# Small products of two heads, issued in turn on the two halves of the TensorE array

## The chip, the cores and the metric

The kernel runs on one core of a Trainium2 chip. The metric is device time in microseconds (us) of one execution; lower is better. Times of before are the median of three executions, and the profile is of one more execution of the same program.

## The reference

A decoder trunk of two layers on 256 tokens of 1024 features, in float32. Layer 0 mixes tokens with four heads of gated linear attention (GLA, chunked, keys of 64, values of 128) and eight heads of sparse attention (DSA: an indexer scores the keys, the best 64 of each token are kept, then softmax attention with a relative bias), and is followed by a dense SwiGLU. Layer 1 mixes with eight FoX heads (softmax attention with a forget bias) and eight dilated heads, and is followed by a SwiGLU of eight experts of which each token takes two. Every sub-layer ends in a norm.

```python
y = x @ w_in                                  # one projection for all heads of a layer
s = einsum('bqhd,bkd->bhqk', q_idx, k_idx)    # DSA indexer, 8 heads of 64
logits = einsum('bqhd,bkhd->bhqk', q, k) * dh ** -0.5 + bias     # 3 x 8 heads of 64
o = einsum('bhqk,bkhd->bqhd', softmax(logits), v)
A = einsum('bhtk,bhsk,bhtsk->bhts', qi, ki, decay)               # GLA within a chunk
x = LN(ALPHA * x + concat(heads) @ w_out)
```

## The kernel before

Every weight matrix is streamed in pieces of up to 1 MB on SP's queue, and ScalarE and VectorE split each piece into two float32r parts (`piece`, L165 and L167). Each large product is then three matmuls, L193 to L195 (`mm3`). The small products of the token mixers work on float32 directly, and every such matmul shows in the trace as two TensorE instructions.

A head has 64 features. Two heads, an even and an odd one, lie above each other in the 128 partitions: the even one in rows 0 to 63, the odd one in rows 64 to 127. So a product over 64 features uses one half of the rows of the array (the trace writes its shape 64\*128), and the two heads of a pair use different halves. The product of the weights with the values contracts over 128 keys and has 64 results, so it uses half of the columns (128\*64).

- `scores` (L538) forms the scores of one head: token tile 0 against 128 keys, token tile 1 against 256 keys, both into one PSUM bank. It is called for each of the 8 heads of the indexer in `dsa_select` (L551) and for each of the 8 heads of the three attentions (L374).
- `attention` (L365) is a generator of eleven steps. Step i forms the scores and the softmax of head i (`weights`: VectorE adds the bias, L666, L749 or L753; maximum L379; exponential L380 and scaling L384 on ScalarE), transposes the weights of head i - 2 (L389, and a ScalarE copy, L391, into one of two buffers `PT`), and multiplies head i - 3 with its values (`values`, L398 and L400). The two heads of a pair share one bank `pos`, which is copied out by `split` (L187, L188) after the odd one. The weights `L` have four buffers.
- `gla_scores` (L427) forms nine sets of products, each for two head pairs d and the two heads a of each: one of q and k themselves, one for b = 128 (L489) and seven levels (L460). `level` does all products of head a = 0 into one bank and copies them out under a mask (L466), then does the same for head a = 1 with another bank.

PSUM has two pools of four banks: `bank` for the large products and `abank` for everything else, so scores, transposes, values and GLA levels share four.

The order on each engine is fixed when the program is built: a planner goes through the instructions with the order of the source as their priority and a timeline of estimated costs, and takes what it holds to be ready, so the small products are put between pieces of large ones. Where a buffer is not yet free, an instruction is put later. The stages of a mixer are woven by hand: `interleave` of the projections with `gla_scores` and `dsa_select` (L650), `weave` of the last projections with GLA's output and the DSA attention (L671, L673), `interleave` of two projections with the FoX attention (L760), and the dilated attention with nothing beside it but the output projection (L766). In `out_proj` the last blocks of token tile 1 are held behind those of tile 0, so that they cover its norm.

Of the kernel before, what the change touches and what calls it, by code (L numbers as in the profile page):

```python
# [18 lines left out]
PSUM = bass.MemoryType.PSUM  # L19
# [3 lines left out]
S = 256  # L23
NT = 2
# [11 lines left out]
# ---------------------------------------------------------------- constants of the shapes  # L36
# [8 lines left out]
def shape_constants():  # L45
    """Masks, permutations and bucket one-hots; none of them depends on the data."""
# [24 lines left out]
def layouts(inputs):  # L71
    """gain and bias of the norm before the router, a feature per partition"""
    cols = np.stack([inputs["ln_g"][1, 0], inputs["ln_b"][1, 0]]).reshape(2, KT, 128).transpose(2, 0, 1)
    return {"ln_cols": np.ascontiguousarray(cols)}
# [13 lines left out]
def interleave(main, side, n=1, m=1):  # L88
    """emit n steps of main, m steps of side, and so on"""
    alive = [True, True]  # L90
    while any(alive):
        for i, g, k in ((0, main, n), (1, side, m)):
            for _ in range(k):
                if alive[i] and next(g, g) is g:
                    alive[i] = False


def weave(pattern, **gens):
    """emit one step of the generator that each letter of the pattern names"""
    for c in pattern:  # L100
        next(gens[c], None)


def lead(n, k):
    """order of the products of n blocks with two token tiles: the first tile ends k blocks before the second"""
# [3 lines left out]
class Trunk:  # L109
# [14 lines left out]
    # ---------------------------------------------------------------- helpers  # L124
    def widen_ring(self, ctx, name, n, later=False):
        """n more buffers for the weights; if later, only once the function that is returned has been called"""
# [15 lines left out]
    def piece(self, src, later=False, cuts=2, raw=None):  # L142
        """Stream one piece of a weight matrix ([128, n, w], or several such side by side) and split it exactly into two float32r parts.
        Returns part(j, columns) -> pair of [128, columns] for the j-th of the n blocks; if later, also a function
        that makes the first part of the i-th of the cuts, which share the blocks evenly, and returns one for the second."""
# [30 lines left out]
    def ring(self, w, dtype=F32):  # L176
        """next buffer of the ring that the weights arrive in"""
# [4 lines left out]
    def rows(self, w, k0, n, c0, c1):  # L182
        """rows k0*128.. of a matrix as [128, n, c1-c0]"""
# [6 lines left out]
    def mm3(self, out, a, b, start, stop):  # L190
        """out += a^T b with a, b pairs of float32r parts"""
# [5 lines left out]
    def proj_t(self, src, evacs, xT):  # L197
        """transposed projection of a piece of columns, up to 128 columns for each of evacs:
        evac(psum [columns, 256 tokens])"""
# [10 lines left out]
    def heads_t(self, w, c0, dst, xT, scale=None, step=2):  # L210
        """transposed projection of all groups of dst ([128, groups, 256]), `step` of them per piece"""
# [4 lines left out]
    def proj_n(self, w, c0, wd, xT, evac):  # L216
        """natural projection of wd (<=512) columns: evac(token tile, psum [128, wd])"""
# [15 lines left out]
    def transposed(self, dst, x, t):  # L233
        """x[:, t] ([128, 1024]) -> dst[:, :, 128 tokens of tile t] (pair of float32r parts)"""
# [8 lines left out]
    def ln_params(self, layer, sub, gb=None):  # L243
        """gain and bias of a norm on all partitions"""
# [7 lines left out]
    def residual_norm(self, x, t, ys, gb, tap=None):  # L252
        """x[:, t] = LN(ALPHA * x[:, t] + y), y given as two halves in PSUM, which are overwritten;
        tap(t, statistics) sees the input of the norm in x[:, t]"""
# [14 lines left out]
    def normalise(self, x, t, st, gb, us, out=None):  # L269
        """x[:, t] = (x - mu) / sqrt(var + eps) * g + b, with the sums of the two halves in st[:, 0:2];  # L270
        us: room for two halves; out: where the result goes to in DRAM"""
# [17 lines left out]
    # ---------------------------------------------------------------- set-up  # L289
# [29 lines left out]
    def router_weights(self):  # L319
        """The router works on z, the input of its norm LN(z) = (z - mu) * rstd * g + b:  # L320
        LN(z) wr = (z (g wr) - mu sum(g wr)) * rstd + b wr, with sums over the features"""
# [16 lines left out]
    def bias_tables(self, m):  # L338
        """Toeplitz bias [128, 8, 256] for the DSA heads and for the dilated heads, t - s = 128 + p - n"""
# [15 lines left out]
    def bias_expand(self, pool, scr, w, name):  # L355
        """T[p, h, n] = row[h, 127 - p + n]"""
# [7 lines left out]
    # ---------------------------------------------------------------- attention  # L364
    def attention(self, qT, kT, v, logits, oT, kt0):  # L365
        """softmax attention of 8 heads of 64; logits(h, S, L) forms the biased and masked logits L from S,
        both [128, 384] = token tile 0 (128 keys) | token tile 1 (256 keys). qT already holds 1/sqrt(d).
        Writes oT[:, kt0:kt0+4] (pair of float32r parts)."""
        nc = self.nc
        blk = (slice(0, 128), slice(128, 384))  # L370
        Ls, PTs, pos = {}, {}, {}

        def weights(h):
            p = self.scores(qT, kT, slice((h % 2) * 64, (h % 2) * 64 + 64), h // 2, h // 2)  # L374
# [18 lines left out]
        def values(h):  # L393
            hp, a = divmod(h, 2)
            if a == 0:
                pos[hp] = self.abank()
            o, PT = pos[hp][a * 64:(a + 1) * 64, :], PTs[h]
            nc.tensor.matmul(o[:, 0:256], v[:, 0, h * 64:(h + 1) * 64], PT[:, 0:256],  # L398
                             start=True, stop=False, skip_group_check=True)
            nc.tensor.matmul(o[:, 128:256], v[:, 1, h * 64:(h + 1) * 64], PT[:, 256:384],  # L400
                             start=False, stop=True, skip_group_check=True)
            if a == 1:
                self.split(oT[0][:, kt0 + hp], oT[1][:, kt0 + hp], pos[hp][:, :S])

        for i in range(8 + 3):
# [4 lines left out]
            if 0 <= i - 3 < 8:  # L410
                values(i - 3)
            yield

    # ---------------------------------------------------------------- GLA
    def logsig(self, z, w, scale=None):
        """log(sigmoid(z)) of a PSUM/SBUF block [128, w] into a new tile"""
# [10 lines left out]
    def gla_scores(self, gaT, q, k, AT, AO):  # L427
        """q, k: [128 (2 heads), 2, 256] transposed; forms A^T (two token tiles) and the off-diagonal block"""
# [22 lines left out]
        def level(X, Y, mask, b):  # L451
            """products of all rows of X with the later halves of the blocks of Y, kept where the mask is set"""
            later = lambda v: v.rearrange("p (m c) -> p m c", c=2 * b)[:, :, b:] if b else v
            n = 64 if b else 128
            for a in range(2):
                r = slice(a * 64, a * 64 + 64)
                p = self.abank()
                for t in range(NT):
                    for d in range(2):
                        nc.tensor.matmul(p[:, (2 * t + d) * n:(2 * t + d + 1) * n],  # L460
                                         X[r, d, t * 128:(t + 1) * 128], later(Y[r, d, t * 128:(t + 1) * 128]),
                                         start=True, stop=True)
# [11 lines left out]
        for i, b in enumerate((128,) + GLA_LEVELS):  # L474
# [9 lines left out]
            if b == 128:  # L484
                for a in range(2):
                    r = slice(a * 64, a * 64 + 64)
                    p = self.abank()
                    for d in range(2):
                        nc.tensor.matmul(p[:, d * 128:(d + 1) * 128], X[r, d, 0:128], X[r, d, 128:256],  # L489
                                         start=True, stop=True)  # L490
                    for d in range(2):
# [5 lines left out]
    def gla_out(self, AT, AO, va, oa):  # L497
        """oa[:, t] = normalised head outputs, before the gate; AT is [s, head % 2, (t, head // 2), t']"""
# [20 lines left out]
    def gla_gate(self, oa, sg, gn, oT):  # L519
        """oT[0:4] = transpose of oa * g_norm * silu(sg), with silu(z) = z (1 + tanh(z/2)) / 2"""  # L520
# [703 lines left out]
```

## Time and profile before

| what | value |
|---|---|
| median of three executions | 1524.82 us |
| lowest and highest | 1524.17 and 1527.38 us |
| span of the profiled execution | 1523.4 us |
| time of the profiled execution outside its span | not recorded; the median is 1.4 us above the span |
| TensorE busy | 1477.5 us (97% of the span) |
| VectorE, ScalarE busy | 1202.6 us (79%), 1028.2 us (67%) |
| layer 0, token mixer | 0 to about 175 us |
| layer 0, dense SwiGLU | about 175 to 375 us |
| layer 1, token mixer | about 375 to 513 us |
| layer 1, experts | about 513 to 1523 us |

The span runs from the first to the last instruction. A matmul's busy time in the profile is longer than the distance to the next one, since they are pipelined: what a block of them costs is read from the start of its first instruction to the start of the next block. TensorE's weight loads are an engine of their own in the trace (PEld).

### The profile page before, as it was taken

How to read it: one execution, taken by the hardware profiler on the slowest of the kernel's cores; microseconds unless marked ns; L12 is line 12 of the kernel's file. 1: busy time of each engine (PE TensorE's matmuls, PEld its weight loads, DVE VectorE, ACT ScalarE, POOL GpSimd, SP SyncE). 2: the span in 40 equal slices, each digit the busy share in tenths (PEclk: the TensorE clock that was granted, in tenths of full speed). 3: DMA queues.
4: the chain of work that ended last, by engine and by line, in shares of the span. 5: the costliest groups of instructions: out<-in, count | busy, mean ns of one | idle time of the engine just before them, and what ended most of it. 6: DMA issues, size and time to landing. Idle time of an engine off the chain costs nothing. (4 is left out here: it accounts for less than half of the span.)

```text
span 1523.4 us, 19538 instructions
## 1 busy us (share of the span) xinstructions
PE 1477.5 (97%) x7226; PEld 1217.4 (80%) x7226; DVE 1202.6 (79%) x1394; ACT 1028.2 (67%) x1328; POOL 92.6 (6%) x85
## 2 busy tenths in 40 slices
PE   6999899998999799999999999999999999999996
PEld 6987688887987688888888888888888887888885
DVE  3687555545554699999999999989979889889987
ACT  3646444433576587878777887877867777677764
POOL 1223300003100220000000000000000000000000
PEclk8999999999999899999999999999999999999998
DMA  8743475555637589999999999999999999999971
GB/s 226 244 137 115 141 244 181 202 176 178 218 86 242 175 293 377 393 357 363 372 333 361 375 375 346 362 342 351 359 359 345 357 362 332 367 351 365 358 271 57
DMA packets 199460, 435.99 MB, mean 286 GB/s; under 512 B 9299, under 2 KB 33659, under 8 KB 199361
## 3 DMA queue, kind: packets, MB, share of 16 engines
q1 hardware_dynamic: 195760, 429.88, 79.2%
q10 hardware_dynamic: 2848, 2.95, 1.0%
q0 software_dynamic: 752, 1.88, 0.5%
q8 instruction: 58, 0.95, 0.3%
q14 instruction: 42, 0.34, 0.1%
HBM read 432.77 MB, written 1.84 MB: 285 GB/s over the span
## 5 line engine op out<-in xcount | busy, mean ns | idle before, releaser
L167 DVE TENSOR_TENSOR wlo<-raw,whi 128x1024 fp32r<-128x1024 f32 (+1 forms) x799 | 953.9, 1230 | 154.5 <-ACT whi L165 135.9
L165 ACT CAST whi<-raw 128x1024 fp32r<-128x1024 f32 (+1 forms) x811 | 821.0, 1045 | 207.3 <-PE bank L195 131.4
L193 PE MATMUL bank<-whi,xgh 128*128 128x512 f32 x896 | 353.8, 396 | 0.0
L194 PE MATMUL bank<-wlo,xgh 128*128 128x512 f32 x896 | 352.3, 393 | 0.0
L195 PE MATMUL bank<-whi,xgl 128*128 128x512 f32 x896 | 351.0, 392 | 0.1
L194 PEld LDWEIGHTS bank<-wlo,xgh 128*128 128x128 f32 x896 | 168.5, 188 | 40.3 <-DVE wlo L167 4.5
L195 PEld LDWEIGHTS bank<-whi,xgl 128*128 128x128 f32 x896 | 168.3, 188 | 36.6 <-ACT xgl L914 0.4
L193 PEld LDWEIGHTS bank<-whi,xgh 128*128 128x128 f32 x896 | 168.5, 188 | 35.6
L194 PE MATMUL y<-wlo,gTh 128*128 128x512 f32 x440 | 173.6, 395 | 0.0
L195 PE MATMUL y<-whi,gTl 128*128 128x512 f32 x440 | 171.5, 392 | 0.7 <-DVE gTl L188 0.7
L193 PE MATMUL y<-whi,gTh 128*128 128x512 f32 x440 | 149.3, 392 | 0.0
L195 PE MATMUL bank<-whi,xTl 128*128 128x512 f32 (+2 forms) x288 | 108.6, 378 | 9.7 <-DVE xTl L188 9.7
L193 PE MATMUL bank<-whi,xTh 128*128 128x512 f32 (+2 forms) x288 | 108.3, 377 | 2.6 <-ACT xTh L187 2.6
L194 PE MATMUL bank<-wlo,xTh 128*128 128x512 f32 (+2 forms) x288 | 107.5, 374 | 0.0
L195 PEld LDWEIGHTS y<-whi,gTl 128*128 128x128 f32 x440 | 82.6, 188 | 18.5 <-DVE gTl L188 1.2
L193 PEld LDWEIGHTS y<-whi,gTh 128*128 128x128 f32 x440 | 82.6, 188 | 17.8
L194 PEld LDWEIGHTS y<-wlo,gTh 128*128 128x128 f32 x440 | 82.7, 188 | 17.7 <-DVE wlo L167 0.3
L187 ACT CAST gTh<-abank 128x512 fp32r<-128x512 f32 (+1 forms) x67 | 38.9, 580 | 73.7 <-PE y L194 53.8
L193 PE MATMUL bank<-xTh,whi 128*128 128x256 f32 (+1 forms) x264 | 77.6, 294 | 6.8 <-ACT whi L165 6.8
L282 POOL TENSOR_TENSOR lnst<-lnst,mhalf 128x1 f32<-128x1 f32 x8 | 4.9, 613 | 1240.1 <-DVE lnst L281 1240.1
L195 PE MATMUL bank<-xTh,wlo 128*128 128x256 f32 (+1 forms) x264 | 77.2, 295 | 0.7 <-DVE wlo L167 0.7
L194 PE MATMUL bank<-xTl,whi 128*128 128x256 f32 (+1 forms) x264 | 77.3, 293 | 0.0
(299 smaller groups left out, 1515.2 us busy)
## 6 DMA issues: line engine op xcount, KB each, us to landing
raw<-in_w_moe SPq DMA_DIRECT2D x333, 1024.0 KB, 6.8
raw<-in_w_dense SPq DMA_DIRECT2D x33, 1024.0 KB, 5.1
raw<-in_w_in_ab SPq DMA_DIRECT2D x13, 1024.0 KB, 11.7
raw<-in_w_in_cd SPq DMA_DIRECT2D x11, 1024.0 KB, 5.4
raw<-in_w_out_ab SPq DMA_DIRECT2D x4, 1024.0 KB, 4.9
raw<-in_w_out_cd SPq DMA_DIRECT2D x4, 1024.0 KB, 5.5
T<-scr_bias ACTq DMA_DIRECT2D x8, 256.0 KB, 9.7
raw<-in_w_moe SPq DMA_DIRECT2D x3, 512.0 KB, 4.3
```

What stands on the lines that cost most here:

```text
L165: nc.scalar.copy(hi, raw[:, sl])
L167: return lambda: eng.tensor_sub(lo, raw[:, sl], hi.bitcast(F32))
L187: self.nc.scalar.copy(hi, src)
L193: mm(out, a[0], b[0], start=start, stop=False, skip_group_check=True)
L194: mm(out, a[0], b[1], start=False, stop=False, skip_group_check=True)
L195: return mm(out, a[1], b[0], start=False, stop=stop, skip_group_check=True)
L282: self.power = nc.gpsimd.tensor_tensor(st[:, 5:6], st[:, 4:5], self.mhalf[:, 0:1], op=OP.pow)
```

## The change

`scores` now takes two banks and issues the products of both heads of a pair in turn: tile 0 of the even head, tile 0 of the odd head, tile 1 of the even head, tile 1 of the odd head. `weights` calls it for every even head and keeps the second bank for the next step; `dsa_select` does the same. `values` is called once for each pair, in the step in which the odd head's values were done before, and issues the even and the odd head's products in turn into the two halves of one bank. `level`, and the product for b = 128, take two banks and issue the products of both heads in turn; the copies under the mask come after both. No product is added or removed, and sizes, operands and the number of buffers stay as they are. Docstrings and comments were removed besides.

```diff
         def weights(h):
-            p = self.scores(qT, kT, slice((h % 2) * 64, (h % 2) * 64 + 64), h // 2, h // 2)
+            if h % 2 == 0:
+                pair[0], pair[1] = self.scores(qT, kT, h // 2, h // 2)
+            p = pair[h % 2]
...
-        def values(h):
-            hp, a = divmod(h, 2)
-            if a == 0:
-                pos[hp] = self.abank()
-            o, PT = pos[hp][a * 64:(a + 1) * 64, :], PTs[h]
-            nc.tensor.matmul(o[:, 0:256], v[:, 0, h * 64:(h + 1) * 64], PT[:, 0:256],
-                             start=True, stop=False, skip_group_check=True)
-            nc.tensor.matmul(o[:, 128:256], v[:, 1, h * 64:(h + 1) * 64], PT[:, 256:384],
-                             start=False, stop=True, skip_group_check=True)
-            if a == 1:
-                self.split(oT[0][:, kt0 + hp], oT[1][:, kt0 + hp], pos[hp][:, :S])
+        def values(hp):
+            po = self.abank()
+            for t, c in ((0, slice(0, 256)), (1, slice(256, 384))):
+                for a in range(2):
+                    h = 2 * hp + a
+                    nc.tensor.matmul(po[a * 64:(a + 1) * 64, t * 128:256], v[:, t, h * 64:(h + 1) * 64], PTs[h][:, c],
+                                     start=(t == 0), stop=(t == 1), skip_group_check=True)
+            self.split(oT[0][:, kt0 + hp], oT[1][:, kt0 + hp], po[:, :S])
...
-            if 0 <= i - 3 < 8:
-                values(i - 3)
+            if 0 <= i - 3 < 8 and i % 2 == 0:
+                values((i - 3) // 2)
...
         def level(X, Y, mask, b):
-            for a in range(2):
-                r = slice(a * 64, a * 64 + 64)
-                p = self.abank()
-                for t in range(NT):
-                    for d in range(2):
-                        nc.tensor.matmul(p[:, (2 * t + d) * n:(2 * t + d + 1) * n],
-                                         X[r, d, t * 128:(t + 1) * 128], later(Y[r, d, t * 128:(t + 1) * 128]),
-                                         start=True, stop=True)
+            ps = [self.abank() for _ in range(2)]
+            for t, d in product(range(NT), range(2)):
+                for a, p in enumerate(ps):
+                    r = slice(a * 64, a * 64 + 64)
+                    nc.tensor.matmul(p[:, (2 * t + d) * n:(2 * t + d + 1) * n],
+                                     X[r, d, t * 128:(t + 1) * 128], later(Y[r, d, t * 128:(t + 1) * 128]),
+                                     start=True, stop=True)
+            for a, p in enumerate(ps):
...
             if b == 128:
-                for a in range(2):
-                    r = slice(a * 64, a * 64 + 64)
-                    p = self.abank()
-                    for d in range(2):
+                ps = [self.abank() for _ in range(2)]
+                for d in range(2):
+                    for a, p in enumerate(ps):
+                        r = slice(a * 64, a * 64 + 64)
                         nc.tensor.matmul(p[:, d * 128:(d + 1) * 128], X[r, d, 0:128], X[r, d, 128:256],
                                          start=True, stop=True)
...
-    def scores(self, qT, kT, r, hp, kp):
-        p = self.abank()
+    def scores(self, qT, kT, hp, kp):
+        ps = [self.abank() for _ in range(2)]
         for t in range(NT):
-            self.nc.tensor.matmul(p[:, t * 128:t * 128 + 128 * (t + 1)], qT[r, hp, t * 128:(t + 1) * 128],
-                                  kT[r, kp, 0:128 * (t + 1)], start=True, stop=True)
-        return p[:, 0:384]
+            for a, p in enumerate(ps):
+                r = slice(a * 64, a * 64 + 64)
+                self.nc.tensor.matmul(p[:, t * 128:t * 128 + 128 * (t + 1)], qT[r, hp, t * 128:(t + 1) * 128],
+                                      kT[r, kp, 0:128 * (t + 1)], start=True, stop=True)
+        return [p[:, 0:384] for p in ps]
...
         for h in range(8):
-            p = self.scores(qiT, ki2, slice((h % 2) * 64, (h % 2) * 64 + 64), h // 2, 0)
+            if h % 2 == 0:
+                ps = self.scores(qiT, ki2, h // 2, 0)
+            p = ps[h % 2]
```

## Rows read from the trace of the kernel before

**Rows 1.** The page: the span, and busy time of each engine.

```profile
span 1523.4 us, 19538 instructions
...
PE 1477.5 (97%) x7226; PEld 1217.4 (80%) x7226; DVE 1202.6 (79%) x1394; ACT 1028.2 (67%) x1328; POOL 92.6 (6%) x85
```

**Rows 2.** Windows cut by stage: stretch and length; busy time (instructions); clock; DMA.

```profile
core 0: us, PE busy (x) PEld busy (x) DVE busy (x) ACT busy (x) POOL busy (x), PEclk, DMA share, GB/s
...
54.50:89.30 34.80, 34.52 (x306) 31.29 (x304) 25.43 (x50) 16.65 (x31) 13.45 (x16) 1.00 0.44 149
...
136.10:163.50 27.40, 27.40 (x129) 18.05 (x128) 12.23 (x28) 16.50 (x45) 4.35 (x6) 1.00 0.35 116
...
419.60:468.30 48.70, 48.70 (x308) 39.13 (x306) 24.67 (x56) 33.34 (x81) 0.00 (x0) 1.00 0.39 109
...
478.80:499.90 21.10, 21.10 (x103) 13.17 (x101) 8.04 (x29) 12.54 (x41) 0.00 (x0) 1.00 0.69 250
499.90:513.00 13.10, 12.18 (x76) 10.51 (x75) 10.03 (x23) 7.41 (x11) 3.79 (x4) 1.00 0.24 80
...
540.00:1523.40 983.40, 970.05 (x4386) 794.04 (x4384) 892.75 (x865) 747.39 (x829) 14.15 (x6) 1.00 0.94 342
```

**Rows 3.** TensorE's timeline, DSA attention: start, duration, line, operands, shape, count.

```profile
140.19 0.39 PE L193 MATMUL bank<-whi,oTh 128*128 128x512 f32 x1
140.43 0.40 PE L194 MATMUL bank<-wlo,oTh 128*128 128x512 f32 x1
140.75 0.92 PE L542 MATMUL abank<-kb,qb 64*128 64x128 f32 x4
141.60 0.43 PE L400 MATMUL abank<-PT,vb 128*64 128x128 f32 x2
...
143.42 0.65 PE L398 MATMUL abank<-PT,vb 128*64 128x256 f32 x2
143.90 0.38 PE L400 MATMUL abank<-PT,vb 128*64 128x128 f32 x2
144.21 0.92 PE L542 MATMUL abank<-kb,qb 64*128 64x128 f32 x4
145.06 0.50 PE L193 MATMUL bank<-whi,oTh 128*128 128x512 f32 x1
145.40 0.40 PE L194 MATMUL bank<-wlo,oTh 128*128 128x512 f32 x1
```

**Rows 4.** TensorE's timeline, first scores of the FoX heads and of the dilated heads.

```profile
419.66 0.93 PE L542 MATMUL abank<-kc,qc 64*128 64x128 f32 x8
420.52 0.38 PE L193 MATMUL bank<-xTh,whi 128*128 128x256 f32 x1
...
468.28 1.57 PE L542 MATMUL abank<-kd,qd 64*128 64x128 f32 x12
469.78 0.50 PE L193 MATMUL bank<-whi,oTc 128*128 128x512 f32 x1
```

**Rows 5.** TensorE's timeline, GLA products, alone and beside scores of the indexer.

```profile
60.84 0.72 PE L489 MATMUL abank<-X 64*128 64x128 f32 x8
61.49 0.39 PE L195 MATMUL bank<-xTh,wlo 128*128 128x256 f32 x1
...
62.27 1.60 PE L460 MATMUL abank<-X 64*128 64x64 f32 x16
63.81 0.39 PE L194 MATMUL bank<-xTl,whi 128*128 128x256 f32 x1
...
76.58 0.27 PE L460 MATMUL abank<-X 64*128 64x64 f32 x1
76.69 0.27 PE L542 MATMUL abank<-ki,qi 64*128 64x128 f32 x1
76.69 0.27 PE L460 MATMUL abank<-X 64*128 64x64 f32 x1
```

**Rows 6.** Waits from 380 to 512 us: total us, times, longest us.

```profile
ACT PT L391 <- PE abank L389: 7.8, 8, 1.8
...
DVE L L753 <- PE abank L542: 5.6, 4, 2.1
```

More of the change, by code (lines that the diff above doesn't have):

```diff
@@ L370, in attention @@
         blk = (slice(0, 128), slice(128, 384))
-        Ls, PTs, pos = {}, {}, {}
+        Ls, PTs, pair = {}, {}, {}
         def weights(h):
-            p = self.scores(qT, kT, slice((h % 2) * 64, (h % 2) * 64 + 64), h // 2, h // 2)
+            if h % 2 == 0:
+                pair[0], pair[1] = self.scores(qT, kT, h // 2, h // 2)
+            p = pair[h % 2]
             L = Ls[h] = self.wk.tile([128, 384], F32, name="L", bufs=4)
@@ L535, in gla_gate @@
             yield
-    def scores(self, qT, kT, r, hp, kp):
-        p = self.abank()
+    def scores(self, qT, kT, hp, kp):
+        ps = [self.abank() for _ in range(2)]
         for t in range(NT):
-            self.nc.tensor.matmul(p[:, t * 128:t * 128 + 128 * (t + 1)], qT[r, hp, t * 128:(t + 1) * 128],
-                                  kT[r, kp, 0:128 * (t + 1)], start=True, stop=True)
-        return p[:, 0:384]
+            for a, p in enumerate(ps):
+                r = slice(a * 64, a * 64 + 64)
+                self.nc.tensor.matmul(p[:, t * 128:t * 128 + 128 * (t + 1)], qT[r, hp, t * 128:(t + 1) * 128],
+                                      kT[r, kp, 0:128 * (t + 1)], start=True, stop=True)
+        return [p[:, 0:384] for p in ps]
     def dsa_select(self, qiT, ki2, wiN, acc):
```

## The prediction

> **What bounds the kernel now.** I read the page first. TensorE is busy for 97% of the span, VectorE for 79%, ScalarE for 67% [rows 1]. That is an average over stages, and a matmul's busy time overlaps that of the next, so I then cut the span into windows by stage [rows 2]. The reader is to see there that in the four stretches in which the touched products run (54 to 89 us GLA and indexer, 136 to 164 us DSA attention, 420 to 468 us FoX, 479 to 500 us dilated) TensorE is busy the whole time (34.5 of 34.8 us, then 27.4 of 27.4, 48.7 of 48.7, 21.1 of 21.1) at full granted clock, and no other engine exceeds 73% of any of them (VectorE 25.4 of 34.8; ScalarE 12.5 of 21.1 in the last). TensorE has no hole there that a shorter product could fall into: time taken off it is taken off the stage, as long as its inputs keep up.
>
> The long last stage, the experts, has TensorE busy for 970 of 983 us and the DMA engines at 94% [rows 2]. It doesn't contain a touched product; I take it to start earlier and keep its length. Its first weights are not late: between the mixer's attention and the experts (499.9 to 513 us) the DMA share is only 0.24, so about 0.76 x 13.1 = 10 us of transfer time is idle there, because the buffers are full [rows 2]. A mixer shortened by some 10 us still finds its weights in place.
>
> **What a small block costs.** The third view is TensorE's timeline. Scores of one head, four instructions, take from 140.75 to 141.60 us: 0.85 us [rows 3]. A large product just before such a block gives way after 0.32 us (140.43 to 140.75) rather than 0.24 (140.19 to 140.43), and the first large one after it takes 0.34 us (145.06 to 145.40): changing shape costs about 0.1 us on each side [rows 3]. A block removed altogether is therefore worth 0.85 to 1.05 us; I take 0.95, since blocks often follow one another and share a border.
>
> **Do two halves of the rows run at once?** Yes, already in this trace. The first two FoX heads happen to be adjacent: eight instructions, 419.66 to 420.52 us, 0.86 us, as long as one head's four. Three dilated heads in a row take 1.50 us (468.28 to 469.78), that is 0.86 for a pair and 0.64 for the third [rows 4]. GLA and indexer products start in the same hundredth of a microsecond (76.69) [rows 5]. So what counts is that the two heads stand next to each other; the turn within the pair matters where one head's run is long.
>
> **The change part by part.** (1) Scores of the three attentions: 24 heads are 12 pairs. Two pairs are adjacent already [rows 4]; 10 single blocks go: 10 x 0.95 = 9.5 us. The indexer's eight heads were called one after the other, stand adjacent in the trace and overlap: nothing.
>
> (2) GLA. One level has 16 instructions, eight for each half, and takes 1.54 us (62.27 to 63.81) [rows 5]. The product for b = 128 has four for each half and takes 0.65 us (60.84 to 61.49): fully overlapped, so its turn changes nothing [rows 5]. Instructions of one half follow each other after 0.11 us (76.58 to 76.69) [rows 5]. Eight for each half in turn are then 0.65 + 4 x 0.11 = 1.09 us, 0.45 less than now. Eight sets (the first one and seven levels): 8 x 0.45 = 3.6 us.
>
> (3) Values. One head's take 0.48 + 0.31 = 0.79 us (143.42 to 144.21) [rows 3], with a border 0.9. The trace has no case of two heads' values next to each other, so whether the two halves of the columns overlap isn't shown. Bounds: if they do not, twelve of 24 borders go, 12 x 0.1 = 1.2 us. If they do, twelve of 24 blocks go, 12 x 0.9 = 10.8 us. The nearest row is that of the other halves, the pair of scores in 0.86 us [rows 4]; by it I take 10.8 and keep 1.2 for the range. By itself: the Trainium skill ("TensorE: Matmul & The Clock Gate", Part 3) gives a speedup of 2.38 for three column tiles with 512 columns; no run here shows it, and by it a pair's 1.58 us would take some 0.8, so that the sum would be within a microsecond of the same.
>
> (4) Sum on TensorE: 9.5 + 3.6 + 10.8 = 23.9 us.
>
> (5) What keeps part of it. In the dilated stage and in the end of the DSA attention little large work is left to put between heads, and TensorE will then wait for the softmax. Two things get later. A pair's values wait for the odd head's transposed weights, and the transposes of the next pair need the two `PT` buffers that only these values free, where before one head's buffer came free at a time; ScalarE's copies into them already wait 7.8 us in eight places, up to 1.8 us each, for the transposes [rows 6]. And VectorE already waits 5.6 us in four places for dilated scores (up to 2.1 us) [rows 6]: these waits shrink, because an odd head's scores are there one step early. The two stretches hold 2 x (2 x 0.95 + 4 x 0.9) = 11.0 us of the sum. If all is kept there, the loss is 0; if nothing is, 11.0. ScalarE is busy for 60% of either stretch (16.5 of 27.4 us, 12.5 of 21.1) [rows 2], so a stretch 5.5 us shorter would have it at 75 to 80%: possible, but not with every wait hidden. I take half, 5 us. In the other two stretches the projections are there as cover, and I take no loss; if GLA's chain (VectorE at 73%) binds instead, 3.6 us more are lost.
>
> (6) Everything else costs nothing: sizes, transfers, copies and their number stay; the second bank's longer life is paid from the four `abank` banks, which is the third rival.
>
> The net is 23.9 - 5 = 19 us. Against the profiled execution, with a span of 1523.4 us, that is 1504.4; its time outside the span isn't recorded, and the median of the runs is 1.4 us above, which I add as what lies around: 1524.8 - 19 = 1506 us.
>
> **The rivals.** *The column halves don't overlap.* For it: no row shows them doing so. Against it: the row halves do [rows 4]. The gain is then 9.5 + 3.6 + 1.2 = 14.3 on TensorE, of which 2 x (1.9 + 0.4) = 4.6 lie in the two tight stretches; half of that lost gives 12 us: 1513 us. *The tight stretches and GLA give nothing*, because the softmax and the mask copies set their pace: 23.9 - 11.0 - 3.6 = 9.3 us, 1515.5 us. Against it: VectorE waits for scores there, not the other way round [rows 6]. I count these two together.
>
> *The planner takes the pairs apart.* It needs two free banks of four at once; where one is free, the even head's products go alone, the odd head's follow later, and the block costs what it does now. The overlap needs adjacency alone, so this undoes the gain pair by pair. If three quarters of the attention pairs are split, what is left is (9.5 + 10.8) / 4 + 3.6 = 8.7 us less some new waits; with GLA's levels split as well and the two tight stretches waiting, nothing: 1522 to 1527 us.
>
> *Banks become the wait (slower).* A pair of scores holds two of four banks from its products until VectorE has read the second, one head later; with a transpose and a pair of values all four are taken, and TensorE, whose order is fixed, stands behind a score that waits for a bank. The head's period in the dilated stage is about 21.1 / 5 = 4.2 us for the five heads scored there after the first three [rows 2, 4], so one such wait can cost up to that, less what large work can be put before it. It decides from 23.9 / 12 = 2.0 us for every attention pair on; at 2.5 us for each, the kernel is at 1524.8 - 23.9 + 30 = 1531 us. Against it: between heads TensorE waits for nothing now [rows 2], and the number of banks taken by a pair of heads is five before and after (two for scores, two for transposes, one for values); the values' bank is even held for less long. The Trainium skill ("TensorEngine Tiling (Array Packing)", section "Gotcha 1: PSUM Pressure") says that row tiling raises the pressure on PSUM, because different row tiles must write different banks. It agrees with the source, where a pair takes two banks; that it costs time, no row here shows.
>
> **How the numbers follow.** Chances: forecast with its partial loss 0.52 (1500 to 1510 us; the lower end is the whole sum, 1524.8 - 23.9 = 1501, less 1 us for shared borders), the two that give half 0.28 (1510 to 1518), the planner 0.12 (1516 to 1527), banks 0.08 (1527 to 1540). The range reaches from 1499, the whole sum with the borders at 1.05 rather than 0.95 us, to 1520, which leaves out the banks and most of the planner's case. A measurement of this kernel tells changes from about 0.2%, 3 us. Faster by more than that, below 1521.8: 0.52 + 0.28 and half of the planner's, 0.86. Within it 0.07, slower 0.07.
>
> **What would show it.** In the profile after, attention scores should stand in blocks of eight of about 0.86 us and GLA levels in blocks of 16 of about 1.1 us. Values in blocks of eight of about 0.8 us would show that column halves overlap; 1.4 to 1.5 us, that they do not. The FoX stretch should be about 6.5 us shorter (3 x 0.95 + 4 x 0.9), GLA's up to 3.6 us, the other two 2 to 5 us each, and the experts' stage should be as long as now. Wrong would be the forecast if scores appear in fours as before, if TensorE shows idle time before scores or transposes that ends on a VectorE read of a bank, or if the experts' stage grows by what the mixers lose.

## The result, and the profile after

The changed kernel takes 1512.93 us (median of 4 runs, 1511.93 to 1513.67) against 1524.9 us for the kernel before, measured beside it: the medians are 12.0 us apart. The ratio estimated from the runs is 0.9914, with a 95% interval of 0.9901 to 0.9926, which is 11 to 15 us. The prediction was 1506 us, with a range of 1499 to 1520: the direction and the range hold, and by the medians the gain is 7 us smaller than the 19 us forecast. The question of this study is where those 7 us went.

The page of the kernel after, to be held against [rows 1]: the same number of instructions on each engine, a span that is 11.6 us shorter, and TensorE still busy for 97% of it.

```profile
span 1511.8 us, 19538 instructions
...
PE 1462.5 (97%) x7226; PEld 1208.5 (80%) x7226; DVE 1201.2 (79%) x1394; ACT 1025.9 (68%) x1328; POOL 91.2 (6%) x85
```

The windows of the kernel after, cut where a stage's first product starts. From the top: GLA, DSA, FoX, dilated, and the experts to the end.

```profile
core 0: us, PE busy (x) PEld busy (x) DVE busy (x) ACT busy (x) POOL busy (x), PEclk, DMA share, GB/s
55.70:108.30 52.60, 51.59 (x414) 45.86 (x414) 44.23 (x107) 26.49 (x44) 13.34 (x18) 0.97 0.43 143
109.30:167.70 58.40, 57.94 (x294) 43.53 (x294) 35.48 (x75) 39.89 (x101) 22.56 (x23) 1.00 0.35 113
413.60:459.20 45.60, 45.60 (x307) 37.06 (x306) 24.45 (x55) 32.46 (x81) 0.00 (x0) 1.00 0.39 116
459.20:492.80 33.60, 33.14 (x174) 23.44 (x174) 18.64 (x55) 22.32 (x66) 0.00 (x0) 1.00 0.69 251
...
510.50:1511.80 1001.30, 987.79 (x4468) 808.88 (x4468) 906.23 (x892) 761.07 (x851) 14.17 (x6) 0.99 0.93 340
```

The kernel before, cut at the same instructions:

```profile
54.60:109.40 54.80, 54.52 (x415) 48.62 (x415) 44.70 (x110) 26.48 (x44) 16.84 (x21) 1.00 0.42 142
110.40:173.30 62.90, 62.90 (x293) 46.03 (x293) 36.56 (x74) 40.83 (x101) 19.25 (x20) 1.00 0.31 103
419.70:468.30 48.60, 48.60 (x307) 39.09 (x306) 24.61 (x55) 33.34 (x81) 0.00 (x0) 1.00 0.39 109
468.30:504.60 36.30, 36.30 (x173) 25.32 (x173) 18.70 (x55) 22.56 (x66) 0.00 (x0) 1.00 0.65 232
...
522.30:1523.40 1001.10, 987.65 (x4468) 808.99 (x4468) 906.41 (x892) 761.05 (x851) 14.15 (x6) 0.99 0.94 340
```

Two things are to be seen. The experts' stage is as long as before (1001.3 and 1001.1 us), so what the mixers save is kept to the end. And TensorE is still nearly without a hole in the attentions: 45.60 of 45.60 us busy in FoX, 57.94 of 58.40 in DSA, 33.14 of 33.60 in the dilated stage, 0.9 us of idle time in all. Most of the gain that is missing is not idle time: TensorE still issues something.

TensorE's timeline of the kernel after, the places that answer to [rows 3 to 5]: start, duration, line, operands, shape, count.

```profile
62.84 1.11 PE L459 MATMUL abank<-X 64*128 64x64 f32 x16
63.88 0.39 PE L194 MATMUL bank<-xTl,whi 128*128 128x256 f32 x1
...
139.95 0.87 PE L401 MATMUL abank<-PT,vb 128*64 128x256 f32 x8
140.75 0.55 PE L391 MATMUL abank<-sq,L 128*128 128x128 f32 x3
...
150.79 0.65 PE L401 MATMUL abank<-PT,vb 128*64 128x256 f32 x2
151.37 0.49 PE L193 MATMUL bank<-whi,oTh 128*128 128x512 f32 x1
...
152.50 0.86 PE L401 MATMUL abank<-PT,vb 128*64 128x256 f32 x6
153.29 0.73 PE L195 MATMUL bank<-whi,oTl 128*128 128x512 f32 x2
...
413.59 0.93 PE L545 MATMUL abank<-kc,qc 64*128 64x128 f32 x8
414.44 0.38 PE L193 MATMUL bank<-xTh,whi 128*128 128x256 f32 x1
...
430.26 0.92 PE L545 MATMUL abank<-kc,qc 64*128 64x128 f32 x4
...
433.69 0.92 PE L545 MATMUL abank<-kc,qc 64*128 64x128 f32 x4
```

The first, second and fifth blocks are what the change is meant to do. A GLA level takes 63.88 - 62.84 = 1.04 us instead of 1.54 [rows 5]. The values of a pair take 140.75 - 139.95 = 0.80 us, as long as one head's 0.79 [rows 3]: the column halves do overlap. Scores of a pair take 0.85 us, as one head's did.

The others are what it does not do. At 150.79 us two instructions of a pair's values (the even head's first product) stand alone, 0.58 us; the other six follow at 152.50, after four large products, and take 0.79 us. Such a pair costs 1.37 us instead of 0.80. At 430.26 and 433.69 us the two heads of one FoX score pair stand 3.4 us apart, each in a block of four. In this trace 9 of the 12 pairs of values are in two pieces, eight of them as "2, then 6", one as "4, then 4". Of the score pairs FoX's last is split, and its third is cut in the middle by two transposes; DSA's last is split as well (four instructions at 141.23 and four at 146.23 us), and in the dilated stage the third is cut by two transposes (two instructions at 471.32 and six at 472.10 us), while the last takes 1.60 us for its eight: the odd head's first product starts 0.75 us behind the even head's (475.69 and 476.44 us). The source issues each pair back to back; the planner that orders TensorE's stream takes them apart.

The waits that the prediction's fifth step was built on, in the kernel after, 373 to 500 us: total us, times, longest us. They answer to [rows 6].

```profile
ACT PT L393 <- PE abank L401: 2.5, 3, 1.5
...
ACT PT L393 <- PE abank L391: 1.0, 2, 0.6
```

ScalarE's copies into the `PT` buffers waited 7.8 us for TensorE's transposes before; now they wait 1.0 us for them and 2.5 us for a buffer that values free. That new wait was foreseen, but it is small.

### The profile page after: what moved, and what is told of

Read it like the earlier page. It is cut to its first block, busy times and chain, and to the rows that moved or that the text cites. A ratio compares the mean times of both kernels' runs of the same rounds, so it can differ in the third digit from the quotient of the medians.

```text
span 1511.8 us, 19538 instructions
## 1 busy us (share of the span) xinstructions
PE 1462.5 (97%) x7226; PEld 1208.5 (80%) x7226; DVE 1201.2 (79%) x1394; ACT 1025.9 (68%) x1328; POOL 91.2 (6%) x85
```

## The experiments

Stage lengths are the evidence throughout. Each is the distance between the first instructions of two stages on TensorE's timeline (GLA: first level to the first product of `va`; DSA: first score to the first transposes of the norm; FoX: first score to the first dilated score; dilated: from there to the router's transposes). The table gives them as the difference to the kernel before, in us, each from one profiled execution; the windows above are the same cuts, rounded. A ratio is estimated from all runs, so it can differ a little from that of two medians.

| kernel | GLA | DSA | FoX | dilated | ratio to before, 95% interval | median us |
|---|---|---|---|---|---|---|
| changed | -2.15 | -4.63 | -3.06 | -2.71 | 0.9914 (0.9901 to 0.9926) | 1512.93 |
| GLA part only | -3.82 | 0.00 | 0.00 | -0.04 | 0.9974 (0.9963 to 0.9984) | 1521.76 |
| scores part only | +0.27 | -2.31 | -2.16 | -2.45 | 0.9956 (0.9943 to 0.9970) | 1519.66 |
| values part only | +0.01 | -0.72 | -0.97 | -2.23 | 0.9977 (0.9968 to 0.9986) | 1522.31 |
| head after head in a pair | +0.01 | -4.68 | -2.05 | -3.37 | 0.9935 (0.9921 to 0.9948) | 1514.98 |
| values tied | -3.65 | -6.02 | -5.55 | -4.04 | 0.9880 (0.9865 to 0.9895) | 1506.20 |
| indexer single | -3.83 | -4.63 | -3.06 | -2.69 | 0.9910 (0.9896 to 0.9923) | 1511.37 |
| tied, FoX banks of its own | -3.64 | -6.02 | -6.93 | -4.25 | 0.9862 (0.9847 to 0.9877) | 1504.54 |
| that, and indexer single | -3.82 | -6.03 | -6.93 | -4.27 | 0.9863 (0.9848 to 0.9878) | 1504.31 |
| tied, own banks, four `PT` | -3.63 | -6.07 | -6.93 | -4.26 | 0.9874 (0.9856 to 0.9891) | 1506.69 |
| changed, once more | -3.66 | -4.63 | -3.06 | -2.71 | one execution, no ratio | 1512.79 |

By the prediction's own terms (0.95 for a score block, 0.9 for a values block) the whole stages should have lost 3.6, 4 x 0.95 + 4 x 0.9 = 7.4, 3 x 0.95 + 4 x 0.9 = 6.45 and 6.45 us before any loss. The prediction's theory for the missing part was waiting for the softmax in the tight stretches; the rival that the profile after suggests is that pairs are taken apart. Letters in an expectation name theories of that expectation.

**One part at a time.** The GLA loops alone:

```diff
-            for a in range(2):
-                p = self.abank()
-                for t in range(NT):
-                    for d in range(2):
+            ps = [self.abank() for _ in range(2)]
+            for t, d in product(range(NT), range(2)):
+                for a, p in enumerate(ps):
```

> The kernel before with the GLA products alone in turn; scores and values as before. Theory A (TensorE bounds the GLA stretch): all of the 3.6 us comes through, ratio about 0.9976. Theory B (the chain of mask copies, exponentials and products on VectorE and ScalarE sets the end of the GLA stretch, as a new 0.9 us wait of TensorE there suggests): about 1 us, ratio 0.9993, with GLA blocks at 1.04 us all the same.

GLA is 3.82 us shorter and nothing else moves: the prediction's 8 x 0.45 = 3.6 us, all kept. The scores alone:

```diff
-            p = self.scores(qT, kT, slice((h % 2) * 64, (h % 2) * 64 + 64), h // 2, h // 2)
+            if h % 2 == 0:
+                pair[0], pair[1] = self.scores(qT, kT, h // 2, h // 2)
+            p = pair[h % 2]
```

> The kernel before with the scores alone in pairs. By the planned order 9 or 10 of 12 attention pairs stand together and 2 or 3 are split, where before 2 pairs did. Theory A (what counts is how many blocks are left): 7 or 8 blocks fewer at 0.95 us, 7 us, less what the DSA and dilated stretches keep: 5 to 7 us, ratio 0.9955 to 0.997. Theory B (the softmax chain sets the pace in the attention stretches): 2 us or less, ratio above 0.9985.

The three attentions give 2.31 + 2.16 + 2.45 = 6.9 us of the 9.5. In this kernel's trace 9 of the 12 pairs stand whole, where 2 did before: seven blocks fewer, 6.65 us at the prediction's 0.95. So splitting alone accounts for what the scores lack (theory A). The values alone:

```diff
-            if 0 <= i - 3 < 8:
-                values(i - 3)
+            if 0 <= i - 3 < 8 and i % 2 == 0:
+                values((i - 3) // 2)
```

> The kernel before with the values alone called for each pair. By the planned order 5 of 12 pairs stand together in eights and 7 are split, the even head's first product alone and the other three later. Theory A (TensorE's time counts): a whole pair gives 0.9 us, a split one 0.2 to 0.3, so 6 us at most and, with half kept by the tight stretches, 4 us: ratio 0.996 to 0.9975. Theory B (values wait for both transposed heads and so delay the next transposes): no gain or a loss, ratio 0.9995 to 1.001.

Values give 0.72 + 0.97 + 2.23 = 3.9 us of 10.8, with 5 of the 12 pairs whole: here is most of what is missing. TensorE's timeline of this kernel, the dilated heads, shows one whole pair and one in two pieces:

```profile
486.75 0.87 PE L399 MATMUL abank<-PT,vd 128*64 128x256 f32 x8
...
490.43 0.65 PE L399 MATMUL abank<-PT,vd 128*64 128x256 f32 x2
491.88 0.86 PE L399 MATMUL abank<-PT,vd 128*64 128x256 f32 x6
```

Of 3.6 us in each attention, the dilated stage, which the prediction held to be tight, keeps most (2.23 us), and FoX, which has the projections as cover and was to lose nothing, keeps 0.97. That speaks against waiting for the softmax as the main cause: four large products stood between the two pieces at 150.79 us in the kernel after, so pieces drift apart where other work is ready. DSA keeps least, 0.72 us, with half its pairs whole; there TensorE does wait once, 0.57 us at 160.87 us, for the transposed weights of an odd head. That is the fifth step's mechanism, in one place.

**The turn within a pair.** All of the even head's products, then all of the odd head's, everywhere; values for example:

```diff
-            for t, c in ((0, slice(0, 256)), (1, slice(256, 384))):
-                for a in range(2):
+            for a in range(2):
+                for t, c in ((0, slice(0, 256)), (1, slice(256, 384))):
```

> The changed kernel with the loops turned: all products of the even head, then all of the odd head, for scores, values and GLA levels; banks and calls as changed. Theory A (adjacency is enough for scores; the turn matters for GLA and for values, where the even head is ready first and runs alone): scores keep their gain, GLA levels are back at 1.54 us, values stand mostly alone; the gain falls from 12 to 6 to 8 us, ratio to before 0.995 to 0.996. Theory B (the turn itself makes the halves overlap): scores blocks of eight take 1.5 us instead of 0.86, and nearly all the gain is lost, ratio 0.998 to 1.

GLA's gain is gone to the hundredth (+0.01), while the attentions keep 4.68 + 2.05 + 3.37 = 10.1 of 10.4 us; stage by stage they differ by up to 1 us. The blocks are as theory A had them, but the gain falls less (0.9935 against 0.995 to 0.996): in this order at least 5 of the 12 pairs of values stand whole, where 3 did in the changed kernel. Its timeline on TensorE:

```profile
62.05 1.60 PE L459 MATMUL abank<-X 64*128 64x64 f32 x16
...
414.52 0.93 PE L545 MATMUL abank<-kc,qc 64*128 64x128 f32 x8
...
428.88 0.86 PE L401 MATMUL abank<-PT,vc 128*64 128x256 f32 x4
...
431.03 0.86 PE L401 MATMUL abank<-PT,vc 128*64 128x256 f32 x4
...
437.42 0.88 PE L401 MATMUL abank<-PT,vc 128*64 128x256 f32 x8
```

Eight values instructions in head-after-head order still take some 0.8 us (437.42), and eight scores 0.93 as before; a level of 16 is back at 1.60. So for runs of four the neighbourhood is enough, as the prediction read it from [rows 4], and the turn matters for runs of eight. Split pairs look different here ("4, then 4") but are split all the same.

**Keeping the values of a pair together.** The odd head's weights are ready last. Its first product is issued first, and the other three are tied behind it:

```diff
+            first = None
             for t, c in ((0, slice(0, 256)), (1, slice(256, 384))):
-                for a in range(2):
+                for a in (1, 0):
...
+                    with self.tc.issue_after(first.ins) if first else nullcontext():
+                        mm = nc.tensor.matmul(...)
+                    first = first or mm
```

> The changed kernel with the four products of a pair of values held together: the odd head's first product is issued first, and the other three only behind it. By the planned order all 12 pairs stand in eights (after: 3 or 4 of 12). Theory A (the planner's pulling apart costs TensorE time): each of 8 split pairs takes 0.80 instead of 1.37 us, 4.6 us; the FoX stretch, which has large work as cover, gets 2 us shorter, DSA and dilated stretches 0.5 to 1 us each; 3 to 4 us less than the changed kernel, ratio to before 0.989. Theory B (the tight stretches are set by the softmax and by the two buffers of transposed weights): FoX alone gains, 2 us, and the dilated stretch gets no shorter or longer.

1506.20 us, 0.9880. DSA, FoX and the dilated stage gain a further 1.39 + 2.49 + 1.33 = 5.2 us. Eight pairs split as "2, then 6", at 1.37 - 0.80 = 0.57 us each, are 4.6 us, and the ninth, whose two pieces took 0.58 and 0.37 us, adds 0.15: the size fits. It is theory A, with more than the 3 to 4 us it had; by B the dilated stage would not have gained. The edit starts with the odd head and ties the rest behind it; the two were not tried apart. TensorE's timeline in FoX:

```profile
425.20 0.87 PE L403 MATMUL abank<-PT,vc 128*64 128x256 f32 x8
...
426.48 0.92 PE L548 MATMUL abank<-kc,qc 64*128 64x128 f32 x4
...
429.55 0.92 PE L548 MATMUL abank<-kc,qc 64*128 64x128 f32 x4
...
432.11 0.87 PE L403 MATMUL abank<-PT,vc 128*64 128x256 f32 x8
```

Values stand in eights (all 12 pairs do); FoX's last score pair still stands in fours, 3.1 us apart.

**The indexer's pairs.** Its scores one head at a time, as before the change:

```diff
-            if h % 2 == 0:
-                ps = self.scores(qiT, ki2, h // 2, 0)
-            p = ps[h % 2]
+            p = self.score1(qiT, ki2, slice((h % 2) * 64, (h % 2) * 64 + 64), h // 2, 0)
```

> The changed kernel with the indexer's scores formed one head at a time as before, so that the GLA levels and the indexer no longer ask for two banks each at once. Theory A (two pairs at once in four banks cost GLA's stretch 1.7 us of what GLA alone gave): the stretch to the end of the values' projection comes back to 3.8 us below before, so 1.5 us less than the changed kernel, ratio to before 0.990. Theory B (the order of the planner there is chance, or other parts cause it): the stretch stays within 0.5 us of the changed kernel.

The attentions don't move and GLA, beside which the indexer runs, comes out at -3.83 instead of -2.15. Read alone, that puts 1.7 us on the indexer's pairs. The tied kernel refutes it: it keeps the pairs and has GLA at -3.65. The runs at the end of this section settle what the first profile had.

**Banks for FoX's scores.** In the tied kernel, both score banks of a FoX pair come from the four banks of the large products:

```diff
-        ps = [self.abank() for _ in range(2)]
+        ps = [(odd or self.abank)() for _ in range(2)]
...
-            fox = self.attention(qc, kc, vc, fox_logits, half(0), 0)
+            fox = self.attention(qc, kc, vc, fox_logits, half(0), 0, self.bank)
```

> As the kernel with tied values, but the FoX scores take both banks from the pool of the large products, so that they no longer compete with transposes and values for four banks. By the planned order all four FoX pairs of scores then stand together, where two were split. Theory A (lack of banks splits the pairs of scores, and each split costs a block): the FoX stretch is 1.5 to 2 us shorter than with tied values. Theory B (the banks are free in time on the chip, or the large products then wait for theirs): no shorter, or longer by up to 1 us. Layer 0 as with tied values in either case.

FoX gains 1.38 us more, to -6.93, a little less than theory A's 1.5 to 2 us; TensorE is busy for 41.68 of 41.68 us there, so the large products don't wait for their banks. 1504.54 us is the best time here together with the next. All four FoX score pairs are whole on TensorE's timeline:

```profile
410.40 0.93 PE L548 MATMUL bank<-kc,qc 64*128 64x128 f32 x8
...
414.32 0.93 PE L548 MATMUL bank<-kc,qc 64*128 64x128 f32 x8
...
418.24 0.93 PE L548 MATMUL bank<-kc,qc 64*128 64x128 f32 x8
...
423.12 0.93 PE L548 MATMUL bank<-kc,qc 64*128 64x128 f32 x8
```

So FoX's score pairs were taken apart for want of small banks: given other banks, they stay together. The Trainium skill ("TensorEngine Tiling (Array Packing)", section "Gotcha 1: PSUM Pressure") says that row tiles must write different banks and so raise the pressure on PSUM; this run agrees and prices it, 1.38 us for one attention, as overlap that is lost and not as a stall. The other two attentions have the output projection on the large banks beside them; this wasn't tried there.

**Both of these,** own banks and the indexer single:

> Tied values, FoX scores in banks of their own and the indexer one head at a time, together. If the three add: 1.5 us less than with tied values and own FoX banks, 6 us less than the changed kernel, ratio to before 0.987. If they disturb one another as the three parts of the change did: 3 to 4 us less than the changed kernel, 0.989.

GLA gains 0.18 us on the kernel with own banks, the total nothing (1504.31 and 1504.54, intervals on top of each other). So the indexer's pairs cost some 0.2 us, not the 1.7 us of the first reading.

**More `PT` buffers.** This is the direct test of the prediction's fifth step, in DSA (layer 1 has no room for them):

```diff
-            PTs[h] = self.pt.tile([128, 384], F32, name="PT", bufs=2)
+            PTs[h] = self.pt.tile([128, 384], F32, name="PT", bufs=4 if self.pt is self.wk and kt0 == 4 else 2)
```

> As the kernel with tied values and own FoX banks, but with four buffers instead of two for the transposed weights of the DSA attention (layer 1 has no room for more). ScalarE's copies into these buffers wait 2.7 us in three places of the DSA stretch for values. Theory A (the two buffers keep part of the sum, as the prediction's step on the tight stretches had it): the DSA stretch, now 6.0 us below before, gets 0.5 to 1.4 us shorter. Theory B (these waits are off the path of TensorE): within 0.2 us of the same; everything else as before in both.

DSA goes from -6.02 to -6.07. The waits in that stretch changed all the same. With two buffers (the kernel with own banks, 107 to 155 us):

```profile
ACT PT L393 <- PE abank L403: 2.7, 3, 1.4
```

With four, that wait isn't listed and only one for the transposes is left:

```profile
ACT PT L393 <- PE abank L391: 1.0, 2, 0.6
```

2.7 us of ScalarE's waiting went and 0.05 us of the stage with it (theory B). The wait exists, off the path that sets the end. The median is 2 us above that of the kernel with own banks, but none of the four stages is longer by more than 0.01 us and the intervals of the ratios overlap.

**The changed kernel once more,** one execution, no edit:

> The changed kernel once more, for its trace. In its first trace the granted clock stood at half from 89 to 92 us, behind a wait of TensorE of 1.2 us at 86 us, and the products up to the end of the values' projection took 1.5 us longer than the same instructions with tied values. Theory A (whether the clock falls behind this wait differs from execution to execution): if the clock stays at full this time, GLA and values' projection together are 3.6 us below before instead of 2.15. Theory B (the order of instructions causes it): 2.15 us again, clock full or not.

The attentions repeat to the hundredth, GLA is -3.66 instead of -2.15. In the first profile of the changed kernel, TensorE's timeline and then VectorE's show this:

```profile
85.91 0.28 PE L194 MATMUL bank<-xTl,whi 128*128 128x256 f32 x1
87.14 1.13 PE L459 MATMUL abank<-X 64*128 64x64 f32 x9 [0.94 <-DVE AT L466]
```

```profile
84.49 1.87 DVE L167 TENSOR_TENSOR wlo<-raw,whi 128x1024 fp32r<-128x1024 f32 x1
86.28 1.27 DVE L466 COPY_PREDICATED AT<-gmask,abank 128x256 f32<-128x256 uint8 x2
```

TensorE waits 0.94 us (1.2 us from the start of the matmul before it) for the mask copy of a level, which stands behind a weight split of 1.87 us on VectorE. The windows of the first profile after that wait, and of the second profile (the column before the last two is the granted clock):

```profile
89.00:93.00 4.00, 4.00 (x21) 3.67 (x20) 3.78 (x13) 1.33 (x4) 0.73 (x2) 0.57 0.44 180
```

```profile
89.00:93.00 4.00, 4.00 (x40) 3.67 (x38) 3.78 (x12) 1.97 (x4) 0.73 (x2) 1.00 0.63 252
```

And TensorE's timeline of the second profile, at the same wait:

```profile
87.93 1.46 PE L459 MATMUL abank<-X 64*128 64x64 f32 x15 [0.94 <-DVE AT L466]
```

The same kernel has the same wait of 0.94 us in both. After it the clock was at 0.57 on average in one execution, most of those 4 us at the lower level, 1.2 GHz; in the other it stayed at 2.4 GHz. In the first, 21 matmuls ran in them; in the second, whose stage lies 0.8 us later, 32 ran from 89.8 to 93.8 us. The difference between the two GLA stages, 3.66 - 2.15 = 1.5 us, goes with the clock of one execution and not with the order of instructions, which is the same. The wait itself comes with the GLA products in turn (the kernel before waits 0.19 us at that level). The six other kernels that have it, 0.94 to 1.07 us long, show the clock at 1.00 from 89 to 93 us, so it fell in one profile of eight; whether the wait brought it down isn't shown.

## Why the prediction was right, and where it was off

The time lies inside the range but outside the favoured 1500 to 1510 us: the range held it because it reached over the rivals. And 1512.9 us is almost the 1513 us of a rival that the trace refutes, column halves that don't overlap. That the two numbers meet is chance; only the blocks on TensorE's timeline tell the causes apart.

*Steps 1 to 3, the sizes.* They hold. Two row halves run at once: 0.85 us for a pair of scores. GLA's levels take 1.04 us, where 1.09 was worked out, and that part is worth 3.6 to 3.8 us. The open point, whether column halves overlap, is decided: 0.80 us a pair, so the 10.8 and not the 1.2 was the right end. The speedup of 2.38 for three column tiles that the prediction took from the Trainium skill ("TensorE: Matmul & The Clock Gate", Part 3) doesn't give the 0.8 us that the prediction drew from it: scaled to two tiles it is 1.59, and a pair would take about 1.0 us (an estimate). The trace, 1.58 / 0.80 = 1.98, shows a fuller overlap.

One reading in front of them is too narrow: "no other engine exceeds 73%" leaves out the weight loads, an engine of their own in the rows, which are busy for 31.29 of 34.80 us in GLA's stretch [rows 2]. They overlap the matmuls, and nothing here hung on it.

*Step 4, the sum.* 23.9 us is about what whole pairs are worth. The best kernel (tied values, FoX banks of its own) has 3.64 + 6.02 + 6.93 + 4.25 = 20.8 us, and FoX, where all pairs are whole, gives 6.93 for the 6.45 worked out.

*Step 5, the loss, is the step that was off, in size and in cause.* It put 5 us of loss on the dilated stretch and the end of DSA, with TensorE waiting for the softmax and two `PT` buffers, and none on FoX. The attentions gave 10.4 of 20.3 us: 9.9 us are missing, FoX with 3.4 of them, where none was expected. TensorE's idle time in them, the form that the step gave to the loss, is 0.9 us. Four `PT` buffers change 0.05 us. Tying the values brings back 5.2 us and own banks 1.4 more: two thirds of the loss is pairs that the planner pulled apart. For FoX's scores it was the want of a second bank. For the values the likely reason is that the even head's weights are ready earlier: the piece that goes alone is its first product, and starting with the odd head's and tying the rest behind it ends the splitting.

*The rivals.* That the column halves don't overlap is refuted. That the planner takes the pairs apart was given 0.12 and a time of 1516 to 1527 us; it is what happened, in part. The prediction had it for banks alone. It did not see that values, which take one bank for the pair, are split more than scores, nor that a split pair still saves something: values at 1.37 us against 2 x 0.79 = 1.58 before. That, and score pairs of which most stayed whole, is why 9 of 12 values pairs split and the result is still 1512.9 us. The rival with banks as the wait is refuted in its form: what banks cost is lost overlap, 1.4 us in FoX with TensorE busy for 45.60 of 45.60 us.

*The other signs named.* Scores in eights, levels in 16: seen where pairs are whole. The experts' stage is 0.2 us longer, where no change was forecast. GLA 2.15 to 3.66 us shorter, DSA 4.6, dilated 2.7 (2 to 5 forecast), FoX 3.06 against 6.5 forecast: the sign that FoX gave was the one that told the cause.

*What stays open.* In the kernel with own banks, DSA keeps 6.0 of 7.4 us and the dilated stage 4.25 of 6.45. DSA's last score pair is still in fours there (139.39 and 144.17 us), worth 0.95 us by the prediction's price of a block, and TensorE waits 0.5 us for a copy of heads' outputs: that would be all of the 1.4. The dilated stage of that kernel shows waits and score blocks that are not whole, 452 to 485 us:

```profile
PEld bank L193 <- ACT oTd L187: 2.3, 4, 1.0
...
PE bank L193 <- ACT oTd L187: 1.2, 2, 0.8
```

```profile
464.25 0.49 PE L548 MATMUL abank<-kd,qd 64*128 64x128 f32 x2
...
465.04 0.92 PE L548 MATMUL abank<-kd,qd 64*128 64x128 f32 x6
...
468.62 1.18 PE L548 MATMUL abank<-kd,qd 64*128 64x128 f32 x8
```

TensorE's weight loads for the output projection wait there for the heads' outputs, 2.3 us; part of that lies behind running matmuls, and TensorE itself is idle for 1.2 us. So once the pairs are whole, some waiting of the kind that step 5 had in mind does show, 1.7 us with DSA's, and not 5. The third score pair, cut by transposes, takes 0.42 + 0.85 us and the last 1.11 us, together 0.66 us more than two at 0.86. That would make 1.9 of the 2.2 us that are missing. None of this was tested.

## What to carry to other kernels

Products that share the array win only as long as they stand next to each other in the stream that is executed, so after pairing them, count the blocks in the trace: source order says nothing when a planner orders the engine. Make a pair one unit by starting it with the product whose input is ready last and tying the rest behind it (5.2 us here), and give it both its banks at once (1.4 us in one stage). A stage with much other ready work isn't safe for pairs: that work is what gets between them.

## What the hardware showed that was not expected

Two heads' values in the two column halves take 0.80 us where one takes 0.79: a full overlap, for the halves of the columns as for those of the rows. The order within the pair is without effect for runs of four instructions a half (a block of eight scores takes 0.86 us in either order, one of eight values 0.81 against 0.80 us) and worth all of the gain for runs of eight (GLA +0.01 against -3.66).

The granted clock after one and the same wait of 0.94 us fell in one execution (0.57 over the 4 us from 89 us on) and not in the other (1.00), at a cost of 1.5 us. A stage length from a single profile can be off by that much, and only a second profile of the same kernel kept it from being put on the indexer.
